# Chains between layers: one accumulator of squares, all elementwise steps on VectorE, the root read from PSUM

## The chip, the cores and the metric

The kernel runs on one core of one Trainium2 chip. The metric is the device time of one execution in microseconds, as the median of several runs.

## The reference, cut to what matters

Eight residual layers work on x of 512 tokens by 1024 features, all in float32: a pooling mixer, a conv-GeGLU feed-forward, a sliding-window attention, a second conv-GeGLU, an S5 state-space mixer, a squared-ReLU MLP, a Mamba-2 (SSD) mixer, a second MLP, and a last norm. What lies between the layers is this:

```
rms_norm(x, g)  = x * rsqrt(mean(x*x over features) + eps) * g
first four:  x = x + rms_norm(m, post_g)       # m: what the mixer or feed-forward gives
             next input = rms_norm(x, pre_g)
last four:   x = x + gate * y                  # gate, shift, scale: from a condition vector
             next input = rms_norm(x, g) * (1 + scale) + shift
```

## The kernel before, in words

x lies feature-major: eight tiles x0 to x7 of 128 features by 512 tokens. Every product is a float32 product taken as three matmuls of parts (`mm3`, lines 219 to 221): high part of the weight with high part of the activation (L219), high with low (L220), low with high (L221). A stage that makes an activation must therefore give two tiles, `hi` (ScalarE) and `lo` (the rest, VectorE). Weights are loaded in chunks and parted in the same way (L204 on ScalarE, L205 on VectorE).

`seam(before, after)` joins two layers in halves of 256 tokens: the last products of the old layer on half 0 (`tail(0)`), the chain of half 0, `tail(1)`, the chain of half 1, and then the first products of the new layer on each half (`head(0)`, `head(1)`). The chains carry a high priority. A planner that simulates the engines makes the order of each engine's queue from the program, the priorities and the waits; engines then run their queues in order.

A chain has these pieces. `Norm.add` squares a tile on ScalarE (L292 the first, L295 the others) and adds it to an accumulator; there are two accumulators, one added to by VectorE and one by GpSimd (L296), and `engs(k)` gives even tiles to VectorE and odd ones to GpSimd. `Norm.rs` sums over partitions with matmuls against ones, both accumulators into one PSUM bank (L306), takes the square root (L309) and the reciprocal (L310), puts it on diagonals (L313), spreads it over all partitions by matmuls into the other half of the bank (L319), and copies it to SBUF (L321, ScalarE). The bank comes from the pool `psn`, which has one.

`post_add` (the first four layers' ends) multiplies each tile by root and gain, `u` (L450 on VectorE; for tiles 2 and 5 a scaling on ScalarE, L442, and a product on GpSimd, L449), adds it to x (L453, alternately on VectorE and GpSimd), and, where the next norm is a `PreScale`, makes the next layer's parts of the new x without waiting for its root: `hi` (L427) and `lo` (L428). The root of `PreScale` is applied later to what the products give. `PreNorm` (before S5, both MLPs and SSD) needs the root first: x times root (L397, alternately VectorE and GpSimd), scale and shift (L400, VectorE), `hi` (L401), `lo` (L402). `staged` takes the eight tiles through these stages, each stage some tiles behind the first: 0, 2, 3, 4 in `post_add` and 0, 1, 1, 3 in `PreNorm`; it also fixes their order on each engine.

During the first seam and the first feed-forward (from about 36 to 460 us) the tables of S5 are made as background work, mostly on GpSimd, with some steps on VectorE, ScalarE and TensorE.

Of the kernel before, what the change touches and what calls it, by code (L numbers as in the profile page):

```python
# [16 lines left out]
ALU = mybir.AluOpType  # L17
# [46 lines left out]
def net_kernel(ctx: ExitStack, tc: tile.TileContext, I: dict, out: bass.AP, parts=ALL):  # L64
# [33 lines left out]
    # ---- constants  # L98
# [62 lines left out]
    # ---- x, feature-major  # L161
# [48 lines left out]
    def chunks(W, k0, nk, c0, ncol=256, kmax=4, gain=None, **kw):  # L210
        """(hi, lo, first k, k tiles) for the rows of k tiles k0.. and columns c0.. of W."""
# [19 lines left out]
    def project(W, k0, nk, c0, tiles, xh, xl, evac, **kw):  # L231
        """Output tiles (an even run of them) over all tokens; evac(n, psum, span)."""
# [8 lines left out]
    class Held:  # L241
        """Output tiles taken over one half of the tokens, then over the other; their weights stay for both.
        runs: (W, k0, nk, c0, apart, kwargs) of one or two tiles each, which share a bank; the weights of the last
        `apart` k tiles lie among the activations."""
# [20 lines left out]
        def run(self, hf, xh, xl, evac):  # L265
            """evac(run, tile of the run, psum, span)"""
# [10 lines left out]
    # ---- root mean square over features (partitions and tiles)  # L277
    class Norm:
        def __init__(self):
            self.acc = {}  # L280
            self.seen = set()

        def add(self, tile_, span, eng):
            a, b = span
            if eng not in self.acc:
                self.acc[eng] = tt("acc")
            dst = self.acc[eng][:, a:b]
            if (eng, a) not in self.seen:
                self.seen.add((eng, a))
                if span == FULL:  # L290
                    self.seen.add((eng, HALVES[1][0]))
# [6 lines left out]
        def rs(self, span, eps, out=None):  # L298
# [3 lines left out]
            accs = list(self.acc.values())  # L302
# [11 lines left out]
            if nb == 2:  # L314
                p2 = ps[:, 256:]
            else:
                p2 = psn.tile([P, 512], F32, tag="n", name=nm("pn"))
            for j in range(nb):
                T.matmul(p2[:, j * P:(j + 1) * P], ones, dg[:, j * P:(j + 1) * P], start=True, stop=True)  # L319
            out = tt("rs") if out is None else out  # L320
            A.activation(out[:, a:b], p2[:, :b - a], AF.Copy)  # L321
# [8 lines left out]
    class Line:  # L330
        """Keeps the instructions given to it in their order on their engine."""
# [1706 lines left out]
```

## Time and profile before

| What | Value |
|---|---|
| median of 3 runs | 2565.32 us (2560.61 to 2565.53) |
| span of the profiled execution, first to last instruction | 2564.4 us |
| the profiled execution's own time | the runs lie 3.8 us below to 1.1 us above its span; no time of its own is listed beside the span |
[...]
| busy share PE, DVE, ACT, POOL | 92%, 66%, 45%, 29% |

PE is TensorE, DVE is VectorE, ACT is ScalarE, POOL is GpSimd. A busy share is an average over stages with different limits; the seams are short, and what happens in them is read from the waits and the timeline there.

### The profile page before, as it was taken

Reading aid. Unit: us, or ns where it says so; the run is one execution under the profiler, and the core shown is the slowest. Engines: PE = TensorE matmul, PEld = TensorE weight load, DVE = VectorE, ACT = ScalarE, POOL = GpSimd, SP = SyncE. Lnnn points to the kernel's source line nnn. Section 1 sums busy time; section 2 is a strip of 40 time slices with the busy share of each in tenths; the row PEclk is TensorE's granted clock in tenths of the full one; section 3 lists DMA queues with packets and bytes.
Section 4 is the critical chain, followed back from the end, with each engine's and each line's share of the span. In section 5 each row is a group of like instructions: output and inputs, shape, how many; then the busy total and the mean of one; then the engine's idle time right before and its main releaser. Section 6 shows DMA issues by size and latency. Waiting matters only on the chain.

```text
span 2564.4 us, 34249 instructions
## 1 busy us (share of the span) xinstructions
PE 2368.0 (92%) x12485; PEld 1989.4 (78%) x12485; DVE 1687.6 (66%) x2739; ACT 1148.0 (45%) x2054; POOL 736.4 (29%) x1111
## 2 busy tenths in 40 slices
PE   6888996998988999996989899999999999999998
PEld 6756674887677888776878787789887888888888
DVE  6874574667857868687653667665778788633333
ACT  6533342447666544343543433334556454423332
POOL 3989988031212000004120201112043332301110
PEclk8988997999999999998989999999999999999999
DMA  4234333222155555652852255553233332233322
GB/s 121 69 98 114 118 121 101 90 80 66 33 155 158 172 181 164 197 164 76 280 180 91 82 171 185 184 172 95 88 113 106 105 98 95 84 98 99 99 86 71
DMA packets 296761, 311.34 MB, mean 121 GB/s; under 512 B 53569, under 2 KB 251025, under 8 KB 295569
## 3 DMA queue, kind: packets, MB, share of 16 engines
q1 hardware_dynamic: 267729, 274.03, 35.2%
q10 hardware_dynamic: 23680, 17.31, 2.2%
q0 software_dynamic: 5184, 17.83, 2.1%
q8 instruction: 98, 1.61, 0.3%
q14 instruction: 70, 0.57, 0.1%
HBM read 284.92 MB, written 24.18 MB: 121 GB/s over the span
## 4 chain that ended last, share of the span: by engine, by line
PE 63%; DVE 12%; POOL 9%; DMA 6%; issue 5%; ACT 4%; SPq 0%; DVEq 0%; ACTq 0%; POOLq 0%
PE mm L220 18%; PE mm L219 18%; PE mm L221 18%; DVE wl L205 3%; DMA as<-in_ada_w 3%; POOL s5buf L659 1%; ACT wh L204 1%; PE pb L1710 1%; DVE u L400 1%; PE mm L1640 1%; PE mm L1641 1%; PE mm L1642 1%; DVE lo L328 1%; PE pn L306 1%; DVE u L450 1%
## 5 line engine op out<-in xcount | busy, mean ns | idle before, releaser
L220 PE MATMUL mm<-h,wh 128*128 128x512 f32 (+1 forms) x1792 | 669.4, 374 | 26.5 <-DVE h L428 13.2
L219 PE MATMUL mm<-h,wh 128*128 128x512 f32 (+1 forms) x1792 | 665.9, 374 | 27.2 <-ACT h L401 11.4
L221 PE MATMUL mm<-h,wl 128*128 128x512 f32 (+1 forms) x1792 | 666.3, 372 | 1.9 <-DVE wl L205 1.9
L205 DVE TENSOR_TENSOR wl<-ws,wh 128x1024 fp32r<-128x1024 f32 (+1 forms) x367 | 499.5, 1365 | 252.2 <-ACT wh L204 239.4
L204 ACT ACTIVATE wh<-ws 128x1024 fp32r<-128x1024 f32 (+1 forms) x367 | 387.2, 1059 | 531.0 <-PE mm L220 435.8
L220 PEld LDWEIGHTS mm<-h,wh 128*128 128x128 f32 x1792 | 348.1, 194 | 86.4 <-DVE h L428 16.9
L219 PEld LDWEIGHTS mm<-h,wh 128*128 128x128 f32 x1792 | 348.1, 195 | 84.1 <-ACT h L401 12.6
L219 PE MATMUL mm<-hi,wh 128*128 128x512 f32 (+1 forms) x1056 | 372.7, 357 | 27.4 <-ACT hi L326 22.3
L221 PEld LDWEIGHTS mm<-h,wl 128*128 128x128 f32 x1792 | 348.7, 195 | 56.8 <-DVE wl L205 2.3
L220 PE MATMUL mm<-lo,wh 128*128 128x512 f32 (+1 forms) x1056 | 373.4, 355 | 11.8 <-DVE lo L328 11.8
L221 PE MATMUL mm<-hi,wl 128*128 128x512 f32 (+1 forms) x1056 | 373.1, 355 | 0.0
L219 PEld LDWEIGHTS mm<-hi,wh 128*128 128x128 f32 x1056 | 201.1, 191 | 55.9 <-ACT hi L326 23.9
L1264 POOL TENSOR_TENSOR r<-r 128x512 f32<-128x512 f32 x64 | 88.0, 1379 | 517.3 <-ACT r L1260 384.2
L220 PEld LDWEIGHTS mm<-lo,wh 128*128 128x128 f32 x1056 | 202.1, 191 | 40.1 <-DVE lo L328 14.2
L221 PEld LDWEIGHTS mm<-hi,wl 128*128 128x128 f32 x1056 | 202.3, 192 | 26.5
L504 DVE SCALAR_TENSOR_TENSOR aa<-as,cond,aa 128x512 f32<-128x512 f32 x168 | 130.1, 774 | 112.8 <-DMA as<-in_ada_w 111.5
L296 POOL TENSOR_TENSOR acc<-acc,sq 128x256 f32<-128x256 f32 (+1 forms) x64 | 62.1, 972 | 389.6 <-ACT sq L295 377.7
L328 DVE TENSOR_TENSOR lo<-r,hi 128x512 fp32r<-128x512 f32 x64 | 48.1, 756 | 76.4 <-ACT hi L326 76.2
L1285 DVE SCALAR_TENSOR_TENSOR x<-mm,mod,x 128x512 f32<-128x512 f32 (+1 forms) x76 | 48.9, 662 | 60.3 <-PE mm L221 60.3
L512 ACT ACTIVATE ab<-aa 128x512 bf16<-128x512 f32 x72 | 45.0, 625 | 90.6 <-DVE aa L504 50.5
L1319 POOL DMA_DIRECT2D vt<-d_tab x16 | 8.8, 555 | 264.7 <-PE mm L221 260.8
L326 ACT ACTIVATE hi<-r 128x512 fp32r<-128x512 f32 x64 | 40.2, 630 | 70.4 <-POOL r L1264 70.3
(494 smaller groups left out, 4084.5 us busy)
## 6 DMA issues: line engine op xcount, KB each, us to landing
ws<-in_mlp_w SPq DMA_DIRECT2D x124, 512.0 KB, 3.9
as<-in_ada_w SPq DMA_DIRECT2D x192, 256.0 KB, 3.1
ws<-in_ffn_w_in SPq DMA_DIRECT2D x88, 512.0 KB, 4.2
ws<-in_m_w_in SPq DMA_DIRECT2D x41, 512.0 KB, 3.7
ws<-in_ffn_w_out SPq DMA_DIRECT2D x40, 512.0 KB, 4.7
ws<-in_w_o SPq DMA_DIRECT2D x16, 512.0 KB, 3.5
ct<-d_tab SPq DMA_DIRECT2D x8, 1024.0 KB, 5.9
ws<-in_s_w_glu SPq DMA_DIRECT2D x16, 512.0 KB, 5.8
```

The lines of the kernel that those rows point to most:

```text
L204: A.activation(h_, s_, AF.Copy)
L205: V.tensor_tensor(l_, s_, f(h_), ALU.subtract)
L219: T.matmul(ps, wh, xh, start=first, stop=False)
L220: T.matmul(ps, wh, xl, start=False, stop=False)
L221: return T.matmul(ps, wl, xh, start=False, stop=last).ins
L296: eng.tensor_tensor(dst, dst, sq[:, a:b], ALU.add)
L326: hi_ = A.activation(hi[:, ts], src, AF.Copy)
L328: return hi_, V.tensor_tensor(lo[:, ts], src, f(hi[:, ts]), ALU.subtract)
L504: V.scalar_tensor_tensor(acc, st, col(k), acc, ALU.mult, ALU.add)
L512: A.activation(parts[j], acc, AF.Copy)
L1264: G.tensor_tensor(r, r, r, ALU.mult)
L1285: V.scalar_tensor_tensor(xT[n][:, ts], ps, md(i, 5, n), xT[n][:, ts], ALU.mult, ALU.add)
```

## The change

Five edits act together. (1) `Norm` keeps one accumulator, added to by VectorE alone, so the sum over partitions takes half as many matmuls. (2) `rs` returns the PSUM half-bank itself; the copy to SBUF stays only for `PreScale`, which keeps its root. (3) `post_add` does all eight products and all eight additions on VectorE, and the scalings of tiles 2 and 5 on ScalarE go. (4) `PreNorm` multiplies by root and scale in one VectorE instruction; the shift becomes the bias of ScalarE's `hi` and is added again in VectorE's `lo`, so that there are three stages instead of four. (5) The lags become 0, 1, 2, 3 and 0, 1, 2. Comments and docstrings go too.

```diff
-POST_LAGS = (0, 2, 3, 4)
-PRE_LAGS = (0, 1, 1, 3)
-POOL_K = (2, 5)
+POST_LAGS = (0, 1, 2, 3)
+PRE_LAGS = (0, 1, 2)
...
-                eng.tensor_tensor(dst, dst, sq[:, a:b], ALU.add)
+                V.tensor_tensor(dst, dst, sq[:, a:b], ALU.add)
...
-                for i, acc in enumerate(accs):
-                    T.matmul(ps[:, j * P:(j + 1) * P], acc[:, a + j * P:a + (j + 1) * P], ones,
-                             start=i == 0, stop=i == len(accs) - 1)
+                T.matmul(ps[:, j * P:(j + 1) * P], self.acc[:, a + j * P:a + (j + 1) * P], ones, start=True, stop=True)
...
-            out = tt("rs") if out is None else out
-            A.activation(out[:, a:b], p2[:, :b - a], AF.Copy)
+            out = ps[:, 256:256 + (b - a)]
             return out
...
-                return engs(k).tensor_tensor(us[k], xT[k][:, ts], rs[:, ts], ALU.mult)
+                return V.scalar_tensor_tensor(us[k], xT[k][:, ts], self.gs[:, k:k + 1], rs, ALU.mult, ALU.mult)
 
             staged((norm,
-                    lambda k: V.tensor_scalar(us[k], us[k], self.gs[:, k:k + 1], md(i, m, k), ALU.mult, ALU.add),
-                    lambda k: A.activation(self.h[k][0][:, ts], us[k], AF.Copy),
-                    lambda k: V.tensor_tensor(self.h[k][1][:, ts], us[k], f(self.h[k][0][:, ts]), ALU.subtract)),
+                    lambda k: A.activation(self.h[k][0][:, ts], us[k], AF.Identity, bias=md(i, m, k)),
+                    lambda k: V.scalar_tensor_tensor(self.h[k][1][:, ts], us[k], md(i, m, k), f(self.h[k][0][:, ts]),
+                                                     ALU.add, ALU.subtract)),
                    PRE_LAGS)
...
-            self.norm.rs(span, self.eps, out=self.rs)
+            A.activation(self.rs[:, slice(*span)], self.norm.rs(span, self.eps), AF.Copy)
...
-        for k in POOL_K:
-            A.activation(ft[k][:, ts], ft[k][:, ts], AF.Copy, scale=vc(gname, g0 + k))
...
-            if k in POOL_K:
-                return G.tensor_tensor(us[k], ft[k][:, ts], rs[:, ts], ALU.mult)
-            return V.scalar_tensor_tensor(us[k], ft[k][:, ts], vc(gname, g0 + k), rs[:, ts], ALU.mult, ALU.mult)
+            return V.scalar_tensor_tensor(us[k], ft[k][:, ts], vc(gname, g0 + k), rs, ALU.mult, ALU.mult)
...
-        staged((norm, lambda k: engs(k).tensor_tensor(xT[k][:, ts], xT[k][:, ts], us[k], ALU.add)) + parts,
+        staged((norm, lambda k: V.tensor_tensor(xT[k][:, ts], xT[k][:, ts], us[k], ALU.add)) + parts,
```

## Rows read from the trace of the kernel before

**Rows 1.** The page: the span, and the chain that ended last by engine.
```profile
span 2564.4 us, 34249 instructions
...
PE 63%; DVE 12%; POOL 9%; DMA 6%; issue 5%; ACT 4%; SPq 0%; DVEq 0%; ACTq 0%; POOLq 0%
```

**Rows 2.** Waits of PE, whole span: us in total, times, longest.
```profile
PE mm L220 <- DVE h L428: 13.2, 10, 2.7
PE mm L220 <- DVE h L402: 13.0, 10, 2.8
...
PE pn L306 <- DVE acc L296: 11.5, 5, 5.7
PE mm L219 <- ACT h L401: 11.4, 5, 2.7
PE mm L219 <- ACT h L427: 11.2, 4, 5.8
```

**Rows 3.** Timeline, seam of first MLP to SSD, half 1: start, us, instructions, idle before.
```profile
1795.35 1.13 PE L306 MATMUL pn<-ones,acc 128*128 128x128 f32 x8
...
1799.91 0.38 ACT L321 ACTIVATE rs<-pn 128x256 f32<-128x256 f32 x1 [3.13 <-PE pn L319]
1801.51 0.42 ACT L401 ACTIVATE h<-u 128x256 fp32r<-128x256 f32 x1 [1.22 <-DVE u L400]
...
1801.98 0.39 PE L219 MATMUL mm<-h,wh 128*128 128x256 f32 x1 [2.17 <-ACT h L401]
1804.19 0.39 PE L220 MATMUL mm<-h,wh 128*128 128x256 f32 x1 [1.82 <-DVE h L402]
```

**Rows 4.** Timeline of PE, seam of second feed-forward to S5, half 1.
```profile
1210.57 2.23 PE L306 MATMUL pn<-ones,acc 128*128 128x128 f32 x8 [5.21 <-DVE acc L296]
```

**Rows 5.** Timeline, seams into attention (half 1) and out of it.
```profile
573.20 0.38 ACT L321 ACTIVATE rs<-pn 128x256 f32<-128x256 f32 x1 [3.48 <-PE pn L319]
573.64 1.16 PE L306 MATMUL pn<-ones,acc 128*128 128x128 f32 x8 [0.53 <-ACT rs L321]
578.92 0.46 PE L220 MATMUL mm<-h,wh 128*128 128x256 f32 x1 [2.52 <-DVE h L428]
...
798.84 2.05 ACT L770 ACTIVATE th<-tz 128x1024 f32<-128x1024 f32 x1 [3.81 <-DMA d_tab<-th]
```

**Rows 6.** VectorE groups by line and shape: busy us, mean ns of one.
```profile
L400 DVE TENSOR_SCALAR u<-u,gs,mod 128x256 f32<-128x256 f32 x64 | 35.6, 564 | 0.3
L450 DVE SCALAR_TENSOR_TENSOR u<-f,vec,rs 128x256 f32<-128x256 f32 x48 | 32.6, 704 | 13.0 <-ACT rs L321 13.0
L296 DVE TENSOR_TENSOR acc<-acc,sq 128x256 f32<-128x256 f32 x62 | 31.7, 514 | 11.1 <-ACT sq L295 9.6
L402 DVE TENSOR_TENSOR h<-u,h 128x256 fp32r<-128x256 f32 x64 | 27.7, 451 | 0.0
L453 DVE TENSOR_TENSOR x<-x,u 128x256 f32<-128x256 f32 x32 | 20.6, 644 | 1.4 <-POOL u L449 1.4
L428 DVE SCALAR_TENSOR_TENSOR h<-x,vec,h 128x256 fp32r<-128x256 f32 x32 | 19.3, 620 | 0.7 <-ACT h L427 0.7
L397 DVE TENSOR_TENSOR u<-x,rs 128x256 f32<-128x256 f32 x32 | 18.6, 583 | 15.7 <-ACT rs L321 15.7
...
L886 DVE SCALAR_TENSOR_TENSOR dl<-mm,vec,dh 128x256 fp32r<-128x256 f32 x16 | 7.7, 479 | 3.2 <-ACT dh L885 2.9
```

**Rows 7.** Timeline of VectorE, pairs back to back, two instructions to a row.
```profile
1175.32 0.74 DVE L976 TENSOR_TENSOR f<-f,mm 128x256 f32<-128x256 f32 x2
...
1784.77 0.86 DVE L1285 SCALAR_TENSOR_TENSOR x<-mm,mod,x 128x256 f32<-128x256 f32 x2
```

**Rows 8.** Timeline of POOL in the first seam: a step of the tables.
```profile
73.50 0.29 POOL L619 TENSOR_TENSOR t<-s5k 128x64 f32<-128x64 f32 x1
```

**Rows 9.** Windows: DVE then POOL busy of L296, of L453; POOL of all lines.
```profile
73.50:96.00 22.50, 2.04 (x3) 2.59 (x4) 0.92 0.00 0
...
73.50:96.00 22.50, 2.55 (x4) 3.64 (x4) 0.92 0.00 0
...
100.00:420.00 320.00, 294.74 (x451) 0.90 0.37 111
```

More of the change, by code (lines that the diff above doesn't have):

```diff
@@ L279, in __init__, with add @@
         def __init__(self):
-            self.acc = {}
+            self.acc = None
             self.seen = set()
-        def add(self, tile_, span, eng):
+        def add(self, tile_, span):
             a, b = span
[L285 to L289, printed above, removed]
+            if self.acc is None:
+                self.acc = tt("acc")
+            dst = self.acc[:, a:b]
+            if a not in self.seen:
+                self.seen.add(a)
                 if span == FULL:
-                    self.seen.add((eng, HALVES[1][0]))
+                    self.seen.add(HALVES[1][0])
                 A.activation(dst, tile_[:, a:b], AF.Square)
@@ L295, in add, with rs @@
                 A.activation(sq[:, a:b], tile_[:, a:b], AF.Square)
[L296 to L298 removed]
+                V.tensor_tensor(dst, dst, sq[:, a:b], ALU.add)
+        def rs(self, span, eps):
             a, b = span
             nb = (b - a) // P
[L302 removed]
             ps = psn.tile([P, 512], F32, tag="n", name=nm("pn"))
             for j in range(nb):
[L305 to L307 removed]
+                T.matmul(ps[:, j * P:(j + 1) * P], self.acc[:, a + j * P:a + (j + 1) * P], ones, start=True, stop=True)
             sr = cst.tile([P, 4], F32, tag="nsr", bufs=2, name=nm("sr"))
@@ L313, in rs @@
                 V.tensor_scalar(dg[:, j * P:(j + 1) * P], ident, sr[:, j:j + 1], None, ALU.mult)
[L314 to L317, printed above, removed]
+            out = ps[:, 256:256 + (b - a)]
             for j in range(nb):
-                T.matmul(p2[:, j * P:(j + 1) * P], ones, dg[:, j * P:(j + 1) * P], start=True, stop=True)
-            out = tt("rs") if out is None else out
-            A.activation(out[:, a:b], p2[:, :b - a], AF.Copy)
+                T.matmul(out[:, j * P:(j + 1) * P], ones, dg[:, j * P:(j + 1) * P], start=True, stop=True)
             return out
@@ L447, in norm @@
             us[k] = tt("u")[:, ts]
-            if k in POOL_K:
-                return G.tensor_tensor(us[k], ft[k][:, ts], rs[:, ts], ALU.mult)
-            return V.scalar_tensor_tensor(us[k], ft[k][:, ts], vc(gname, g0 + k), rs[:, ts], ALU.mult, ALU.mult)
+            return V.scalar_tensor_tensor(us[k], ft[k][:, ts], vc(gname, g0 + k), rs, ALU.mult, ALU.mult)
         parts = pre.parts(span) if pre is not None else ()
-        staged((norm, lambda k: engs(k).tensor_tensor(xT[k][:, ts], xT[k][:, ts], us[k], ALU.add)) + parts,
+        staged((norm, lambda k: V.tensor_tensor(xT[k][:, ts], xT[k][:, ts], us[k], ALU.add)) + parts,
                POST_LAGS[:2 + len(parts)])
         for k in range(KD):
-            nxt.add(xT[k], span, engs(k))
+            nxt.add(xT[k], span)
     def reduce_angle(a, k):
@@ L912, in tail_ @@
                     A.activation(ft[n + q][:, a:b], o, AF.Copy, scale=vc("pool_scale", n + q))
-                    sq.add(ft[n + q], (a, b), engs(q))
+                    sq.add(ft[n + q], (a, b))
             if hf == 0:
@@ L977, in down @@
                 if last:
-                    S_["sq"].add(ft[n], span, engs(n))
+                    S_["sq"].add(ft[n], span)
         def body_():
@@ L1142, in o_proj @@
                     A.activation(ft[n + q][:, slice(*HALVES[th])], o, AF.Copy)
-                    S_["sq"].add(ft[n + q], HALVES[th], engs(q))
+                    S_["sq"].add(ft[n + q], HALVES[th])
         def head(hf, pre):
@@ L1286, in down @@
             if nxt is not None:
-                nxt.add(xT[n], span, engs(n))
+                nxt.add(xT[n], span)
             bg[0](1)
@@ L1426, in glu @@
             if S_["nxt"] is not None:
-                S_["nxt"].add(xT[n], span, engs(n))
+                S_["nxt"].add(xT[n], span)
         def body_():
@@ L1666, in o_evac @@
             if S_["nxt"] is not None:
-                S_["nxt"].add(xT[n], span, engs(n))
+                S_["nxt"].add(xT[n], span)
         def bcast(a, o, d=64):
@@ L1893, in chain @@
             for k in range(KD):
-                nxt.add(xT[k], span, engs(k))
+                nxt.add(xT[k], span)
     work = Background()
```

2 lines of the change are left out of this document (removed).

## Prediction

> **What bounds the kernel now.** I read first the page's chain of waits: TensorE carries 63% of it and stands at 92% busy, VectorE 12% and POOL 9% [rows 1]. So over most of the span only matmul work counts, and nothing of that changes. The change can be worth no more than the places where TensorE stands still for a chain between layers. The second view, the waits of TensorE alone, gives their size: 13.2 us for `lo` and 11.2 for `hi` of the parts made behind `post_add`, 13.0 for `lo` and 11.4 for `hi` of `PreNorm`, 11.5 for the accumulator of squares, together 60.3 us in 34 waits [rows 2]. That is the most that shorter chains can remove directly, 2.4% of the span.
>
> The third view is the timeline of one seam, half 1 of MLP to SSD [rows 3]. The reader is to see the order: sum matmuls, then the root's copy to SBUF at 1799.91, the first `hi` at 1801.51, TensorE's first product at 1801.98, and its second, which needs the first `lo`, only at 1804.19. TensorE is idle 2.17 + 1.82 us of these 4.3. So what ends last is the first `lo`, and that is VectorE's: before it stand products, scalings and waits for GpSimd's share. The fourth view, the groups by line, shows what the two engines do to each other: VectorE's plain additions and products have means of 514 to 704 ns in the lines that run beside GpSimd, while the same shapes back to back, with GpSimd idle, take 0.37 us (two in 0.74) and, with a scalar pointer, 0.43 us (two in 0.86) [rows 6, 7].
>
> **The change part by part.** The base is the profiled execution, 2564.4 us; the median of the runs lies 0.9 us above, which I add at the end.
>
> *PreNorm.* Removed are the copy of the root (0.38 us), the separate scaling, and GpSimd's products. In the new order VectorE does product 0, 1, 2 and then `lo` 0: with 0.43 us for each product and 0.48 for the last, 1.8 us, and 0.1 for the hand-over, 1.9 us from the point at which the copy now starts [rows 6, 7]. ScalarE's `hi` 0 takes 0.42 us now [rows 3]; even if its new bias makes it half as long again, it ends 0.43 + 0.1 + 0.63 = 1.2 us on, before the turn of `lo` 0 at 1.3. Against 4.3 us now the gain is 2.4 us a half. Five halves wait like this, as the count of the `hi` row says, and a sixth (SSD to second MLP) for `lo` alone [rows 2]: 6 x 2.4 = 14.4 us. What comes after the first `lo` stays as it was: a tile now costs VectorE 2 x 0.43 = 0.86 us, before half a product and two others at 0.37, 0.93. The lower bound is that the later tiles set the end, at 8 x 0.07 = 0.6 us plus the 0.4 of the copy, 1.0 a half, 6 us; the upper is all of both `PreNorm` rows, 24.4.
>
> The product now reads the root from PSUM, and no row shows that product. The nearest is L886, the same instruction with an operand in PSUM, at 479 ns [rows 6], and L1285's pair in rows 7, also from PSUM; I take them, and so charge nothing more. [...]
>
> *post_add.* With lags 0, 1, 2, 3 VectorE does four products (1.72 us), three additions (1.11) and `lo` 0 (0.48): 3.3 us from the root. Into attention it is 5.7 now, from 573.20 to 578.92 [rows 5], so 2.4 us for this half. Out of attention the longest wait for `hi`, 5.8 us [rows 2], is not GpSimd's: ScalarE's queue stands behind a copy of the S5 tables that waits 3.81 us for a DMA [rows 5]. Nothing of the change touches that, so between 0 and 2.4 I take 1.2. The first half into attention I put at nothing, since `head` work covers most of it. Sum 3.6; bounds 0 and 24.4, the rows' whole.
>
> *Second feed-forward to S5* has `post_add` and `PreNorm` one behind the other, so the whole first chain is bare. TensorE waits 5.21 us for the accumulator and then takes 2.23 us for eight sum matmuls, four of which go [rows 4]: 1.1, and 0.4 for the copy, 1.5 a half, 3.0 for both. VectorE's additions that were GpSimd's I put at nothing, since GpSimd's ended no earlier; the bound is all 11.5 us of rows 2.
>
> *Sums of squares elsewhere.* Eight sum matmuls take 1.13 us [rows 3], half of it goes: 0.5 us in the six other halves counted above, 3.0. Where TensorE would have waited anyway it is nothing: 0 to 3.
>
> *VectorE's load.* This is the cover of all that, so it has to be checked. The seven lines of rows 6 without L886 cost VectorE 186.1 us. After the change there are, by the program's loops, 128 products, 96 `lo` with a pointer among those lines, 64 additions to x and 148 to accumulators (168 squares less 20 first ones). At 0.43 and 0.37: 224 x 0.43 + 212 x 0.37 = 175 us. VectorE takes over all of GpSimd's share and yet ends no fuller, if the means of rows 6 fall to rows 7's. If they stay, 224 x 0.62 + 212 x 0.51 = 247 us, 61 more, and half of that in waits would eat the gains.
>
> *First seam.* The chain of waits runs on POOL from there to 416 us: POOL is busy 294.74 of the 320 us after 100 [rows 9], and TensorE waits for its tables in the first feed-forward. So I count nothing for this seam's own waits, but what GpSimd loses of it once the tables' steps have begun, at 73.50 [rows 8]: 2.59 us of accumulating and 3.64 of additions [rows 9], 6.2 us. Against it, VectorE's own table steps, which must come first, stand behind more chain work of high priority: I take 2 us off and keep 4.2; bounds -6 and 10. No queue of SP or POOL gets a new DMA, and no DMA moves.
>
> Sum: 14.4 + 3.6 + 3.0 + 3.0 + 4.2 = 28.2 us. 2564.4 - 28.2 = 2536.2, and with 0.9, **2537 us**.
>
> **The rivals.** *The bank is held.* The root now lies in the only bank of its pool until the eighth product has read it: eight products, some six additions and four `lo` later, 8 x 0.43 + 6 x 0.37 + 4 x 0.43 = 7.4 us, where the copy freed it after 0.4. In the three seams with `PreScale` the next root's sums stand right behind: into attention they started at 573.64, 0.53 us behind the copy, ahead of the new layer's products in TensorE's queue [rows 5]. If the planner leaves them there, TensorE waits 7.4 us where 3.3 would have done: 4 us more in three seams, 12 us, and the time is 2549. Against it: the planner sees the wait and can queue the products first.
>
> *The chains end sooner than TensorE's other waits show.* Waits shorten by more, because with GpSimd gone nothing doubles VectorE's instructions (means of 514 to 704 against 370 and 430): twice the two first terms, 18 us more, and 2519.
>
> *Slower: the tables lose their pace.* Every queue is planned anew. POOL's work from 100 to 420 us is on the chain; it idles 25 us there [rows 9]. If VectorE's and ScalarE's steps for it come later in their queues, because chain work goes ahead, its idle time grows and each microsecond is one of the kernel's. This decides above 24 us of new idle time, the sum without the first seam: about twice what it idles now. At 35 the time is 2565.3 - 24 + 35 = 2576.
>
> **How the numbers follow.** The forecast, with its own range 2526 to 2547: 0.52. The held bank (2547 to 2558): 0.18. The larger gain (2508 to 2526): 0.16. The tables' loss, slower: 0.11; the same with a loss that just cancels: 0.03. A difference under 0.2%, 5 us, is about what a measurement of this kernel can't tell from none. Of the held bank nearly all is still faster. So faster 0.84, same 0.05, slower 0.11. The range goes from 2510, where half of all 60 us is gone and the tables gain too, to 2559, which takes in the held bank and leaves out the tables' loss.
>
> **What would show it.** Right: TensorE's waits for `lo` behind `PreNorm` shrink from 13.0 to under 6, the first `lo` comes some 2 us after the spread of the root, VectorE's chain lines have means near 0.4 to 0.5 us, and the sum matmuls stand four to a root instead of eight. Wrong for the first seam: POOL's work on the tables does not end earlier. The held bank would show as a wait of the sum matmuls for the last product. The prediction is wrong as a whole if VectorE's means stay at 0.5 to 0.7 without GpSimd beside it, or if TensorE's idle time moves from the seams into the first feed-forward.

## The result, and the profile after

The changed kernel takes 2526.39 us (median of 4 runs, 2522.45 to 2528.71) against 2563.69 us of the kernel before beside it: a ratio of 0.9855, 95% interval 0.9841 to 0.9868, so 37 us or 1.45% faster. The forecast was 2537 us, in a range of 2510 to 2559.

The page of the changed kernel, its span and the chain of waits by engine. VectorE has the same share as in [rows 1]; POOL fell from 9% to 7%.

```profile
span 2525.6 us, 33954 instructions
...
PE 66%; DVE 12%; POOL 7%; DMA 6%; issue 4%; ACT 4%; SPq 0%; DVEq 0%; ACTq 0%; POOLq 0%
```

TensorE's waits over the whole span (us in total, times, longest). They answer to [rows 2]: L392 and L391 are the remainders and rounded parts of `PreNorm` (13.0 and 11.4 before), L419 and L418 those behind `post_add` (13.2 and 11.2 before), L303 the sum matmuls (11.5 before). L312 are the matmuls that spread the root; in the kernel before their row is the last one here.

```profile
PE pn L303 <- DVE acc L295: 17.8, 2, 9.4
PE pn L312 <- DVE dg L309: 12.2, 8, 4.4
...
PE mm L218 <- ACT h L418: 8.0, 4, 2.4
...
PE mm L219 <- DVE h L419: 7.5, 10, 1.4
PE mm L218 <- ACT h L391: 7.0, 6, 1.5
...
PE mm L219 <- DVE h L392: 3.1, 5, 1.2
```

```profile
PE pn L319 <- DVE dg L313: 2.5, 3, 1.0
```

The reader is to see three things. The four rows for rounded parts and remainders fell from 48.8 us to 25.6. The wait for the accumulator grew by 6.3, and that for the diagonals, which no term of the forecast has, by 9.7. Together these rows went from 62.8 us to 55.6. So most of the gain is not in the waits that these rows list, and TensorE's idle and busy time have to be looked at as a whole. The pages have them, before and then changed:

```profile
PE 2368.0 (92%) x12485; PEld 1989.4 (78%) x12485; DVE 1687.6 (66%) x2739; ACT 1148.0 (45%) x2054; POOL 736.4 (29%) x1111
```

```profile
PE 2346.8 (93%) x12397; PEld 1970.7 (78%) x12397; DVE 1686.3 (67%) x2839; ACT 1143.1 (45%) x2022; POOL 611.5 (24%) x967
```

Of the 38.8 us between the two profiled executions TensorE's idle time gives 17.6 (196.4 to 178.8) and its busy time 21.2. The busy time fell for two reasons. There are 88 sum matmuls fewer, four in each of 22 roots; at 1.13 us for eight and 0.61 for four, as the seam below has them, that is an estimate of 11 us. And the mean granted clock rose from 0.962 to 0.967: by the trace's clock records TensorE did 128 us of its work at the lower of the two levels that they hold, 0.50 of full speed and 1.00, before and 104 now, 109 in a second execution told of below. In the kernel before, 128x256 matmuls start 0.21 us apart at 0.50 (13 steps from 1436.16 to 1438.93) and 0.12 apart at 1.00 (13 from 1440.02 to 1441.58), so some 0.44 of that difference, an estimate of 8 to 11 us, is what it is worth. The clock is not that of one execution alone: the runs of the kernel before beside the later experiments have 0.959 to 0.962, the eight of the changed kernel 0.965 to 0.969. Span and mean granted clock of the two profiled executions, before and then changed:

```profile
core 0: 2564.4 us, clock 0.962
```

```profile
core 0: 2525.6 us, clock 0.967
```

The timeline of the seam from the first MLP to SSD, half 1, as in [rows 3]:

```profile
1764.60 0.61 PE L303 MATMUL pn<-ones,acc 128*128 128x128 f32 x4
...
1766.18 0.68 PE L312 MATMUL pn<-dg,ones 128*128 128x128 f32 x4 [0.96 <-DVE dg L309]
1766.90 1.26 DVE L388 SCALAR_TENSOR_TENSOR u<-x,gs,pn 128x256 f32<-128x256 f32 x3 [0.67 <-PE pn L312]
1767.41 1.30 ACT L391 ACTIVATE h<-u,mod 128x256 fp32r<-128x256 f32 x3 [1.90 <-DVE u L388]
...
1767.97 0.39 PE L218 MATMUL mm<-h,wh 128*128 128x256 f32 x1 [1.11 <-ACT h L391]
...
1768.61 0.39 PE L219 MATMUL mm<-h,wh 128*128 128x256 f32 x1 [0.25 <-DVE h L392]
```

From the point where the root is there to TensorE's second product it was 4.28 us (1799.91 to 1804.19) and is 1.71 (1766.90 to 1768.61). From the start of the sums to that product it was 8.84 and is 4.01; but in the kernel before TensorE had products of the other half to do between sums and spread, so that difference is not all idle time.

The timeline of the seam from the second feed-forward to S5, half 1, against [rows 4]: the spread of `post_add`'s root, VectorE's additions, and the sum matmuls. The wait for the accumulator is 9.40 us, where it was 5.21.

```profile
1185.53 0.60 PE L312 MATMUL pn<-dg,ones 128*128 128x128 f32 x4
...
1192.34 3.06 DVE L295 TENSOR_TENSOR acc<-acc,sq 128x256 f32<-128x256 f32 x6
...
1195.54 1.20 PE L303 MATMUL pn<-ones,acc 128*128 128x128 f32 x4 [9.40 <-DVE acc L295]
```

The spread of the same root in the kernel before:

```profile
1200.45 0.60 PE L319 MATMUL pn<-dg,ones 128*128 128x128 f32 x4
```

VectorE's groups by line (busy us, mean ns), against [rows 6]. The means of products and additions to x have fallen from 583 to 704 ns to 438 to 474.

```profile
L295 DVE TENSOR_TENSOR acc<-acc,sq 128x256 f32<-128x256 f32 (+1 forms) x148 | 63.7, 443 | 16.2 <-ACT sq L294 11.9
...
L392 DVE SCALAR_TENSOR_TENSOR h<-u,mod,h 128x256 fp32r<-128x256 f32 x64 | 29.9, 479 | 0.2 <-ACT h L391 0.2
L434 DVE SCALAR_TENSOR_TENSOR u<-f,vec,pn 128x256 f32<-128x256 f32 x64 | 29.6, 472 | 7.5 <-PE pn L312 7.5
L388 DVE SCALAR_TENSOR_TENSOR u<-x,gs,pn 128x256 f32<-128x256 f32 x64 | 29.0, 474 | 9.1 <-PE pn L312 9.1
L437 DVE TENSOR_TENSOR x<-x,u 128x256 f32<-128x256 f32 x64 | 28.0, 438 | 0.0
L419 DVE SCALAR_TENSOR_TENSOR h<-x,vec,h 128x256 fp32r<-128x256 f32 x32 | 16.4, 518 | 1.1 <-ACT h L418 1.1
```

The first seam: the step of the tables that [rows 8] has at 73.50, the VectorE step that it waits for, and a later pair of the tables.

```profile
66.21 0.21 DVE L597 TENSOR_TENSOR s5k<-s5k,t 128x64 f32<-128x64 f32 x1
66.50 0.41 POOL L603 TENSOR_TENSOR t<-s5k 128x64 f32<-128x64 f32 x1 [8.28 <-DVE s5k L597]
...
82.64 2.35 POOL L709 TENSOR_TENSOR cp<-cc,s5k 128x512 f32<-128x512 f32 x2
```

In the kernel before:

```profile
68.13 5.40 POOL L296 TENSOR_TENSOR acc<-acc,sq 128x256 f32<-128x256 f32 x4 [1.98 <-ACT sq L295]
70.37 0.21 DVE L613 TENSOR_TENSOR s5k<-s5k,t 128x64 f32<-128x64 f32 x1
...
95.80 2.18 POOL L725 TENSOR_TENSOR cp<-cc,s5k 128x512 f32<-128x512 f32 x2
```

The pair stood at 95.80 and stands at 82.64, so the tables are 13.2 us ahead: 7.0 by an earlier start, 6.2 because nothing of the chain lies between. The earlier start has two parts. VectorE's step comes 4.2 us sooner (70.37 to 66.21), and behind it GpSimd's step waited 3.1 us for the four additions of squares that stood in GpSimd's queue, where now it starts within 0.3.

**Where the time came from.** For each VectorE and ScalarE instruction that stands in both programs (the n-th of its line) I took how much earlier it starts than in the kernel before; the gain at a point is the median over those within 15 us of it, and a stretch's gain the difference of two points. The forecast's terms stand with the stretch of their halves. The fourth column is a second profiled execution of the changed kernel, the other three are runs told of below. All in us; the ends of the stretches are times in the kernel before.

| stretch | forecast | changed | again | spare additions | four stages | sums on TensorE |
|---|---|---|---|---|---|---|
| first seam and first feed-forward, to 540 | 4.2 | 13.0 | 13.2 | 3.9 | 13.0 | 19.8 |
| into attention, to 610 | 2.9 | 4.3 | 4.6 | 5.5 | 5.6 | 7.9 |
| attention, out of it, second feed-forward, to 1150 | 1.7 | -1.4 | -8.8 | -5.8 | -6.5 | 0.4 |
| into S5, to 1250 | 7.8 | 1.5 | 2.5 | 1.5 | -0.5 | 12.6 |
| S5, to 1395 | 0 | 4.0 | 6.3 | 6.0 | 4.9 | 1.6 |
| S5 to first MLP, to 1500 | 5.8 | 8.2 | 8.0 | 8.3 | 3.2 | 6.1 |
| first MLP, to 1740 | 0 | 1.9 | 0.3 | -0.5 | -2.0 | -0.4 |
| first MLP to SSD, to 1850 | 2.9 | 5.0 | 5.7 | 4.9 | 4.6 | 5.2 |
| SSD, to 2150 | 0 | -0.9 | -5.1 | -1.3 | 0.9 | -3.0 |
| SSD to second MLP, to 2320 | 2.9 | 3.3 | 3.3 | 3.2 | -1.4 | 0.9 |

The seams agree between the two executions of one program within 1 us. The stretches that the change does not touch differ by up to 7.4 us, so a seam's row can be read to about a microsecond, and the others say little.

TensorE's idle time in a stretch is steadier; in the four seams below the two executions differ by 0.2 us at most. It is the length less TensorE's busy time, in us, the ends of a stretch moved by each run's gain at that point, and stands here for the four seams with `PreNorm`, in the kernel before, the changed kernel, and the runs told of below. In the three seams behind S5 it fell by 9.0 us, of the 16.5 that the table above gives them; the rest is busy time.

| run | into S5 | S5 to first MLP | first MLP to SSD | SSD to second MLP |
|---|---|---|---|---|
| before | 20.8 | 8.6 | 5.3 | 4.6 |
| changed | 21.9 | 3.9 | 2.5 | 3.1 |
| again | 21.9 | 3.9 | 2.3 | 3.1 |
| GpSimd's share back | 15.9 | 3.9 | 1.9 | 3.2 |
| root copied | 23.4 | 4.4 | 3.0 | 4.7 |
| four stages | 23.7 | 6.5 | 3.2 | 5.4 |
| old lags | 22.3 | 4.7 | 2.7 | 4.0 |
| two accumulators | 18.7 | 4.2 | 2.3 | 3.1 |
| root whole | 23.6 | 6.2 | 3.5 | 4.2 |
| sums on TensorE | 9.4 | 6.1 | 3.7 | 4.7 |
| root by place | 9.4 | 3.9 | 2.4 | 3.1 |

### The profile page after: what moved, and what is told of

Read it like the earlier page. It is cut to its first block, busy times and chain, and to the rows that moved or that the text cites. A ratio compares the mean times of both kernels' runs of the same rounds, so it can differ in the third digit from the quotient of the medians.

```text
span 2525.6 us, 33954 instructions
## 1 busy us (share of the span) xinstructions
PE 2346.8 (93%) x12397; PEld 1970.7 (78%) x12397; DVE 1686.3 (67%) x2839; ACT 1143.1 (45%) x2022; POOL 611.5 (24%) x967
## 4 chain that ended last, share of the span: by engine, by line
PE 66%; DVE 12%; POOL 7%; DMA 6%; issue 4%; ACT 4%; SPq 0%; DVEq 0%; ACTq 0%; POOLq 0%
PE mm L219 20%; PE mm L218 19%; PE mm L220 19%; DVE wl L204 3%; DMA as<-in_ada_w 2%; ACT wh L203 1%; PE mm L1624 1%; PE mm L1625 1%; DMA d_tab<-s5buf 1%; PE mm L1626 1%; POOL s5buf L642 1%; POOL s5buf L644 1%; PE pb L1694 1%; DVE aa L488 1%; POOL s5buf L643 1%
## 5 line engine op out<-in xcount | busy, mean ns | idle before, releaser
L219 PE MATMUL mm<-h,wh 128*128 128x512 f32 (+1 forms) x1792 | 665.3, 372 | 11.1 <-DVE h L419 7.5
L204 DVE TENSOR_TENSOR wl<-ws,wh 128x1024 fp32r<-128x1024 f32 (+1 forms) x367 | 479.5, 1309 | 254.0 <-ACT wh L203 239.0
L488 DVE SCALAR_TENSOR_TENSOR aa<-as,cond,aa 128x512 f32<-128x512 f32 x168 | 131.5, 783 | 109.0 <-DMA as<-in_ada_w 107.7
L295 DVE TENSOR_TENSOR acc<-acc,sq 128x256 f32<-128x256 f32 (+1 forms) x148 | 63.7, 443 | 16.2 <-ACT sq L294 11.9
```

The source lines that it names most:

```text
L204: V.tensor_tensor(l_, s_, f(h_), ALU.subtract)
L219: T.matmul(ps, wh, xl, start=False, stop=False)
L295: V.tensor_tensor(dst, dst, sq[:, a:b], ALU.add)
L488: V.scalar_tensor_tensor(acc, st, col(k), acc, ALU.mult, ALU.add)
```

## The experiments

Ratios are to the kernel before, beside which each ran.

**The changed kernel again.** No edit.

> The changed kernel once more, word for word, as a second execution under the profile and a base on the same chip for the others: 2526 us within 4. Where a stage that no edit touches (the feed-forwards' bodies, S5's body, attention) differs between the two profiles by 2 us, such a difference elsewhere says nothing about an edit. If instead the stages agree within 1 us, differences of 2 us and more between kernels come from the new order of the queues.

Measured: 2533.18 us against 2568.13, ratio 0.9868 (0.9852 to 0.9884). The time is 7 us above the first, outside the 4 expected; the kernel before is 4.4 us slower beside it too, and the ratios agree. The two profiles agree within 0.3 us until 540 us and end 8.8 us apart (the bottom of the table's columns adds to 38.9 and 30.0), so the first reading holds: differences of a few us inside the bodies say nothing. Where the second execution loses most, from 610 to 1150 us of the kernel before, TensorE is idle 3.5 us longer and busy 4.1 us longer, and the granted clock of the stretch is 0.97 where the first has 0.98. Part of the idle time goes with longer waits for weights: between 880 and 1010 us VectorE waits 24.4 us for them (L488) where the first has 21.8.

For the other runs I take 0.9862, between the two ratios of the changed kernel, as the base; 0.0010 is 2.6 us, and a run's interval is some 0.0016 to either side.

**GpSimd's share back, everywhere.** `eng` is `engs` of the tile, and each engine has an accumulator of its own.

```diff
-                V.tensor_tensor(dst, dst, sq[:, a:b], ALU.add)
+                eng.tensor_tensor(dst, dst, sq[:, a:b], ALU.add)
...
+    def engs(k, first=False):
+        return G if k % 2 and (True if first else True) else V
...
-    staged((norm, lambda k: V.tensor_tensor(xT[k][:, ts], xT[k][:, ts], us[k], ALU.add)) + parts,
+    staged((norm, lambda k: engs(k, first).tensor_tensor(xT[k][:, ts], xT[k][:, ts], us[k], ALU.add)) + parts,
```

> The changed kernel with GpSimd's odd share back in every seam: additions to x and additions of squares of odd tiles, with a second accumulator and eight sum matmuls a root instead of four. PreNorm's stages, the products of post_add and the root in PSUM stay as changed. Theory (the share that left GpSimd is worth something only ahead of the tables and in the sum matmuls; the seams gain by their shorter chains on VectorE): the first seam gives back about 12 us, the sums 3 us, and the second feed-forward to S5 gains up to 7 us, since its two accumulators run side by side (TensorE's wait for the accumulator falls from 9.4 us to about 5): 2526 + 15 - 7 = 2534 us. Rival (the two engines slow each other, and that was the larger part of the gain in all seams): the lines of VectorE go back to means of 500 to 700 ns and all but the folded stages is lost, 2526 + 25 = 2551 us or more.

Measured: 2541.47 us, ratio 0.9897 (0.9884 to 0.9910), some 9 us slower than the changed kernel, between the theory's loss of 8 and the rival's of 25. The profile has both signs: the first feed-forward ends 9.8 us later than in the changed kernel (gain there 3.2 us), and into S5 it gains 5.1 us instead of 1.5, with the shorter wait that was expected. The rival's sign shows too, in part: of VectorE's groups the additions of squares go to a mean of 549 ns (514 before, 443 changed) and the remainders behind `post_add` to 730 (620 and 518), but the products, which read PSUM, stay at 472 and 474. TensorE's row for the accumulator, whole span:

```profile
PE pn L306 <- DVE acc L296: 11.5, 2, 6.4
```

**The same share back in the first seam alone.** The edit is shown against the run before it.

```diff
-        return G if k % 2 and (True if first else True) else V
+        return G if k % 2 and (True if first else False) else V
```

> The changed kernel with GpSimd's odd share (additions to x and of squares, second accumulator) back in the first seam alone, between the pooling layer and the first feed-forward. Theory (GpSimd's queue: this share stood among the tables' steps, and the tables set the end until they are done): the tables' first steps start late again and all of it is lost later, some 12 of the 38.8 us: 2538 us, with the loss complete by 222 us of the span. Rival (the prediction's own term, 4.2 us): 2530 us. Rival (the first seam gained by the shorter chain on VectorE, not by GpSimd's queue): no change, 2526 us.

Measured: 2530.50 us, ratio 0.9859 (0.9847 to 0.9872): no loss in the time. In the profile the loss is there by 540 us, 3.3 us gained instead of 13.0; it then gains 6.1 into attention and 3.3 from there to 840, where the changed kernel has 4.3 and -2.1. So the stage reading was right, and the expected loss of 12 us in the time did not come.

**Spare additions on GpSimd in the first seam.** VectorE's chain stays as changed; GpSimd adds in place, on squares and products that are already used.

```diff
                 V.tensor_tensor(dst, dst, sq[:, a:b], ALU.add)
+                if extra:
+                    spare(sq[:, a:b])
...
+    def spare(src):
+        G.tensor_tensor(src, src, src, ALU.add)
...
+            if first and k % 2:
+                spare(us[k])
```

> The changed kernel with extra additions on GpSimd in the first seam, as many and as large as its share there before (additions of odd squares and to odd tiles of x), whose results nobody reads; VectorE's chain is as changed. Theory (GpSimd's queue: these instructions stand ahead of and among the tables' steps): by the end of the first feed-forward (540 us) 7 to 10 us of the gain there of 12.5 us are lost, as in the run with GpSimd's share back in the first seam. Rival (that run lost by the longer chain through two engines): by 540 us at most 2 us are lost, and the time is 2526 us.

Measured: 2540.39 us, ratio 0.9898 (0.9881 to 0.9915), 9 us slower. By 540 us 3.9 us are gained instead of 13.0. VectorE waits for none of their results, so the rival falls: the loss needs no longer chain through two engines. POOL's timeline, the same two steps as above:

```profile
69.78 0.41 POOL L615 TENSOR_TENSOR t<-s5k 128x64 f32<-128x64 f32 x1 [0.56 <-DVE s5k L609]
...
96.56 4.15 POOL L721 TENSOR_TENSOR cp<-cc,s5k 128x512 f32<-128x512 f32 x2
```

The pair is back at 96.56, near where the kernel before has it. Of the 13.9 us, 10.6 lie between the two steps, in GpSimd's queue, which is more than the 6.2 that the kernel before had there; 3.3 are a later start. That start is VectorE's: the step that this one waits for also comes 3.3 us later than in the changed kernel (69.48 against 66.21). Why this run keeps the loss to the end and the one before it does not is open.

**The root copied.**

```diff
-            out = ps[:, 256:256 + (b - a)]
+            p2 = ps[:, 256:256 + (b - a)]
...
+            out = tt("rs")[:, a:b] if out is None else out
+            A.activation(out, p2, AF.Copy)
             return out
```

> The changed kernel with the root copied to SBUF by ScalarE again, ahead of the products of PreNorm and post_add. Theory (the copy stood bare on the chain): 0.4 us for each of 8 halves of PreNorm and some 4 of post_add, 2526 + 3 to 5 = 2530 us. Rival (the root's bank, held until the eighth product, costs as much in sums that wait for it as the copy): 2526 us, and TensorE's waits for the spread of the next root get shorter. Second rival (a product that reads PSUM takes longer): means of the product lines fall below those of the changed kernel and the time is 2524 us.

Measured: 2536.42 us, ratio 0.9882 (0.9868 to 0.9897), about 5 us slower by the ratio, as the theory had it, though its interval overlaps that of the changed kernel's second measurement. TensorE's idle time bears it out: 4.1 us more in the four seams with `PreNorm`. The second rival falls by VectorE's groups: the two products, now from SBUF, have the means of the changed kernel, 484 and 478 ns against 472 and 474.

```profile
L436 DVE SCALAR_TENSOR_TENSOR u<-f,vec,rs 128x256 f32<-128x256 f32 x64 | 30.4, 484 | 8.6 <-ACT rs L314 8.6
L390 DVE SCALAR_TENSOR_TENSOR u<-x,gs,rs 128x256 f32<-128x256 f32 x64 | 29.3, 478 | 11.8 <-ACT rs L314 11.8
```

**Four stages again.**

```diff
-    V.scalar_tensor_tensor(us[k], xT[k][:, ts], self.gs[:, k:k + 1], rs, ALU.mult, ALU.mult)
+    V.tensor_tensor(us[k], xT[k][:, ts], rs, ALU.mult)
...
+    lambda k: V.tensor_scalar(us[k], us[k], self.gs[:, k:k + 1], md(i, m, k), ALU.mult, ALU.add),
-    lambda k: A.activation(self.h[k][0][:, ts], us[k], AF.Identity, bias=md(i, m, k)),
+    lambda k: A.activation(self.h[k][0][:, ts], us[k], AF.Copy),
...
-               PRE_LAGS)
+               (0, 1, 1, 3))
```

> The changed kernel with PreNorm's four stages and their lags 0, 1, 1, 3 as before (product with the root, scale and shift, rounded part, remainder), but all of VectorE's on VectorE. Theory (the fold is what brought the first remainder forward): eight instructions of 0.4 us stand ahead of and with the first remainder instead of four, 1.7 us more for each of 6 to 8 halves and TensorE waits for the remainder again as in the kernel before: 2526 + 10 to 14 = 2538 us. Rival (the move away from GpSimd did it, the fold little): 2528 us.

Measured: 2547.14 us, ratio 0.9922 (0.9908 to 0.9936), 15 us slower: the largest of the single steps. In the table 2 to 3 us are lost into S5, 5 from S5 to the first MLP, 4.7 from SSD to the second MLP. TensorE's idle time in the four seams with `PreNorm` is 7.4 us longer. The clock has a share in the rest: in the last of these seams 0.98 is granted, where the changed kernel has 1.00. TensorE's waits, whole span, `PreNorm` only (7.0 and 3.1 in the changed kernel):

```profile
PE mm L218 <- ACT h L392: 10.0, 6, 1.9
PE mm L219 <- DVE h L393: 8.0, 9, 1.8
```

**The old lags.**

```diff
-POST_LAGS = (0, 1, 2, 3)
-PRE_LAGS = (0, 1, 2)
+POST_LAGS = (0, 2, 3, 4)
+PRE_LAGS = (0, 1, 3)
```

> The changed kernel with every later stage one tile further behind: lags 0, 2, 3, 4 in post_add and 0, 1, 3 in PreNorm, so that another product stands ahead of the first remainder. Theory (the order of the queue sets the first remainder): 0.4 us more in each of 8 halves of PreNorm and some 4 of post_add, 5 us, 2531 us, with TensorE's waits for remainders up by as much. Rival (VectorE's rate over all eight tiles sets the end, not the first remainder): 2526 us.

Measured: 2541.44 us, ratio 0.9887 (0.9870 to 0.9904), 6.5 us slower, near the theory's 5, with an interval that overlaps the changed kernel's second one. TensorE's idle time in the four seams with `PreNorm` grows by 2.3 us only. `PreNorm`'s wait for remainders rises from 3.1 to 5.8 us; the rows behind `post_add` show no such rise, so the whole of it is not accounted for.

The four single steps that were undone cost 9, 5, 15 and 6.5 us, together 36 us, about what the changed kernel gains. That they add up so well is in part luck. Each figure has an interval of some 4 us to either side; the four stages and the old lags both set the remainder back by the same lag; GpSimd's share brings the second accumulator and its sum matmuls with it; and GpSimd's products, in `PreNorm` and for tiles 2 and 5, were not undone at all.

**Two accumulators, both VectorE's, into S5.** `two` is set there alone.

```diff
+            w = k % 2 if self.two else 0
-            dst = self.acc[:, a:b]
+            dst = self.acc[w][:, a:b]
```

> The changed kernel with two accumulators between the second feed-forward and S5, both VectorE's, odd and even tiles apart, and eight sum matmuls a root there. Theory (additions into one accumulator take longer because each waits for the one before it: six in 3.0 us, 0.51 us each, against 0.37 us for two that are independent): six take 2.2 us and TensorE's wait for the accumulator falls from 17.8 to about 16 us; the sums give most of it back, 2526 us within the noise. Rival (the additions take that long because of the squares that they read, or of other work): the spacing stays at 0.5 us and the wait at 17.8.

Measured: 2536.81 us, ratio 0.9871 (0.9855 to 0.9888), no change, as expected. The mechanism shows in VectorE's timeline of half 0, and in TensorE's wait:

```profile
1161.92 0.76 DVE L296 TENSOR_TENSOR acc<-acc,sq 128x256 f32<-128x256 f32 x2
1165.71 1.43 DVE L296 TENSOR_TENSOR acc<-acc,sq 128x256 f32<-128x256 f32 x4
```

```profile
PE pn L306 <- DVE acc L296: 14.6, 2, 7.8
```

Four additions into two accumulators take 1.43 us, 0.36 each; six into one took 3.06, 0.51 each. The wait falls by 3.2 us, and eight sum matmuls (2.05 us instead of 1.20) give part of it back. The time between the spread of `post_add`'s root and the sums, half 1, is 8.37 us (1187.11 to 1195.48), where the changed kernel has 10.01.

**The root made whole.** A version that goes further, since the waits for the accumulator and the diagonals were now the longest of the chains.

```diff
-            for j in range(nb):
-                T.matmul(ps[:, j * P:(j + 1) * P], self.acc[:, a + j * P:a + (j + 1) * P], ones, start=True, stop=True)
...
+            T.matmul(ps[:, :b - a], ones, self.acc[:, a:b], start=True, stop=True)
+            out = tt("rs")[:, a:b] if out is None else out
+            A.activation(out, ps[:, :b - a], AF.Sqrt, bias=eps, scale=1.0 / D)
+            V.reciprocal(out, out)
```

> The changed kernel with the root made on all partitions at once: one sum matmul with the ones as the weight gives every token's sum on all 128 partitions, ScalarE takes the square root of 128 x 256 from PSUM into SBUF and VectorE its reciprocal there; the two scaled diagonals and the matmuls that spread them go, and the products read SBUF. Theory (after the change, what ends last in the seams is the root's own chain: TensorE waits 12.2 us for diagonals and the path from the sums to the spread is some 2.2 us): about 1 us off in each of 10 to 12 halves, 2526 - 10 = 2516 us, and no waits for diagonals. Rival (a reciprocal over 256 columns costs VectorE as much as the steps it replaces): 2526 us. Second rival (it costs 2 us and more): 2535 us.

Measured: 2521.86 us against 2533.18 of the changed kernel on the same chip; ratio 0.9825 (0.9809 to 0.9840). The 11 us are the theory's, but not in the places it named. The seams of `PreNorm` alone get worse: 6.4, 4.5 and 1.3 us gained over the kernel before, where the changed kernel has 8.2, 5.0 and 3.3; TensorE is idle 4.4 us longer in them. The gain lies ahead of them, 17.8 us by 540 and 7.6 into attention; what of it is the earlier free bank and what the new order of the queues was not tried.

**The sums on TensorE, into S5.**

```diff
+            if self.bank is not None:
+                sq = tt("sq")
+                A.activation(sq[:, a:b], tile_[:, a:b], AF.Square)
+                T.matmul(self.bank[:, :b - a], ones, sq[:, a:b], start=k == 0, stop=k == KD - 1)
+                return
```

> As the run with the whole root, and between the second feed-forward and S5 the squares of the new x are summed by TensorE, eight matmuls into one bank, in place of VectorE's chain of additions into one accumulator. Theory (the single accumulator is what kept this seam from gaining: its additions follow each other at 0.5 us and TensorE waited 17.8 us for it, 11.1 before): the wait falls under 10 us, this seam gains 4 to 7 us over the run with the whole root, 2510 us. Rival (the products and the additions to x end last there, the accumulator only follows them): under 2 us, 2515 us.

Measured: 2514.35 us, ratio 0.9792 (0.9777 to 0.9807), 7.5 us better than the run with the whole root. Into S5 it gains 12.6 us, where that run gains 3.7. TensorE's waits in that seam (1115 to 1200 us), and VectorE's group of the reciprocals:

```profile
PE mm L218 <- ACT h L390: 6.8, 2, 3.4
PE pn L287 <- ACT sq L286: 2.3, 2, 1.4
```

```profile
L311 DVE RECIPROCAL rs<-rs 128x256 f32<-128x256 f32 x16 | 28.0, 1751 | 36.5 <-ACT rs L310 36.5
```

The rival falls: the wait of 17.8 us for the accumulator has become one of 2.3 for squares. Not all of the gain is that wait, though: TensorE, with the sums to do, is idle 9.4 us in this seam instead of 23.6, and the granted clock of the stretch is 0.96, where the run with the whole root has 0.86. What each of the two is worth was not separated. The 1751 ns of the reciprocal is what stands bare in the other seams.

**The root by place.** `PreNorm`'s three seams without `post_add` go back to diagonals.

```diff
-            rs = self.norm.rs(span, self.eps)
+            rs = self.norm.rs(span, self.eps, whole=self.norm.bank is not None)
```

> The run with the sums on TensorE, but PreNorm's root in the three seams without post_add (S5 to the first MLP, MLP to SSD, SSD to the second MLP) made by diagonals again, as in the changed kernel; elsewhere the root is made whole. Theory (the 1.75 us that the reciprocal over 128 x 256 takes stands bare in those three seams, where the path by two diagonals is shorter): those seams go back from 6.1, 2.9 and 1.2 us gained over the kernel before to the changed kernel's 8.1, 5 and 3.2: 6 us, 2514 - 6 = 2508 us. Rival (the diagonals' two small steps and their hand-overs cost as much as the reciprocal): 2514 us.

Measured: 2513.59 us, ratio 0.9782 (0.9767 to 0.9797). The three seams gain 7.5, 5.0 and 3.2 us instead of 6.1, 5.2 and 0.9, which is 3.5 us and not 6, and the time does not tell this run from the one before. TensorE's idle time falls by 5.1 us there, as the theory has it, and is that of the changed kernel again. It is the fastest measured: 2.2% under the kernel before and, by the ratios 0.9862 and 0.9782, 0.8% under the changed kernel.

## Why the prediction was right in sum, and where its terms were wrong

The forecast sum was 28.2 us and the gain 36 to 37, inside the range. That it came so near is in part luck: the first seam gave 9 us too much, the seam into S5 6 us too little, and an estimated 8 to 11 us go with the clock, for which the forecast has no term. Term by term:

*PreNorm, right in mechanism, with the sums too small and the clock left out.* Forecast: 1.9 us from the root to the first remainder's product; measured 1.71, a gain of 2.57 us against 2.4. The run that undoes the fold alone costs 15 us, most of it in these seams. In the three seams of `PreNorm` alone TensorE's idle time fell by 9.0 us, where four halves of 2.4, 9.6, were forecast. It is not 2.4 in each: in half 1 of MLP to SSD the idle time behind the sums fell from 3.99 us to some 2.5, as TensorE now waits 0.96 for the diagonals, where products of the other half had covered that path. But the three seams gained 16.5 us, where 11.6 were forecast with the sums. What is left is busy time. The sum matmuls were counted in eight halves at 0.5 to 1.1 us; they went in all 22, and count wherever TensorE is the bound, an estimate of 11 us in all against the 5.2 of the sum. The rest goes with the clock: in the three seams 0.95, 0.98 and 0.99 of full speed were granted before (1395 to 1500, 1740 to 1850 and 2150 to 2320 us), and 0.98, 0.98 and 1.00 are in the same stretches of the changed kernel.

The half from 1425 us of the kernel before, in the seam from S5 to the first MLP, shows it. Behind two waits of 1.82 and 1.72 us it went on in part at the lower of the clock's two levels, 0.50 from 1436 to 1439 us and 0.89 in the mean of 15 us; the same half of the changed kernel waits 1.11 us ahead of its products and the granted clock stays at 1.00. The windows (PE, PEld, DVE, ACT, POOL busy, clock, DMA), before and then changed:

```profile
1425.00:1440.00 15.00, 11.45 (x79) 10.84 (x79) 9.07 (x23) 4.85 (x14) 3.29 (x4) 0.89 0.00 1
```

```profile
1403.00:1418.00 15.00, 13.75 (x110) 13.30 (x110) 9.39 (x21) 8.41 (x17) 1.38 (x1) 1.00 0.05 8
```

The same is seen inside S5, where nothing of the change lies and 4.0 us were gained. The stretch, before and then changed:

```profile
1250.00:1395.00 145.00, 132.56 (x769) 117.53 (x768) 75.32 (x90) 62.41 (x84) 23.39 (x35) 0.94 0.59 186
```

```profile
1232.60:1373.60 141.00, 128.76 (x766) 113.98 (x765) 78.06 (x93) 62.16 (x84) 20.32 (x33) 0.96 0.60 192
```

TensorE is idle 12.4 and 12.2 us; the 4 us are busy time, at a clock of 0.94 and 0.96. The second execution has 0.98 there and gains 6.3; the run with the root by place has 0.94 and gains nothing. So the gain inside S5 goes with the clock. Why the clock stood higher there is open.

*The first seam: 4.2 us forecast, 13 found, beyond the upper bound of 10.* The failed step is "what GpSimd loses of it once the tables' steps have begun, at 73.50". It counted the 6.2 us of chain work behind that point, which the trace confirms to the tenth, and nothing ahead of it; but the start itself went from 73.50 to 66.50. Of these 7.0 us, 2.8 are GpSimd's additions of squares that stood ahead of the step, and 4.2 are VectorE's own table step, for which the forecast had taken 2 us off: it came earlier, not later. The spare additions show that work in GpSimd's queue takes the gain back, without a longer chain. How much of the 9 us reaches the end is less sure, since one of the two runs that take it back lost it and the other did not.

*Into S5: 7.8 us forecast, 1.5 and 2.5 found.* The failed step is "VectorE's additions that were GpSimd's I put at nothing, since GpSimd's ended no earlier". Two engines had summed side by side; now VectorE does all seven after its products, and each waits for the last, six of them 0.51 us apart. TensorE's wait went from 11.5 us, nearly all of it in this seam, to 17.8: 6.3 more, by which the term falls short. The chain itself did not get longer in half 1: from the spread of `post_add`'s root to the sums it took 10.12 us (1200.45 to 1210.57) and takes 10.01 (1185.53 to 1195.54). What the copy and the shorter instructions gave back, the additions took; and the wait grew because 4.3 us of TensorE's work that had stood behind the spread now stand ahead of it. In half 0 the same stretch grew from 14.96 us (1166.20 to 1181.16) to 17.35 (1149.73 to 1167.08). Three runs show from three sides that the accumulator is what is waited for: GpSimd's half back, 11.5; two accumulators, 14.6; sums on TensorE, 2.3. What the new order of TensorE's queue alone costs was not tried.

*post_add: right in sign.* Into attention 2.9 us with the sums, found 4.3 and 4.6. Out of attention nothing can be read, since that stretch differs more between two executions of one program than the term's 1.7 us.

*VectorE's load: wrong, without effect.* The lines of the chain cost 186.1 us before and 196.6 now (63.7, 29.9, 29.6, 29.0, 28.0 and 16.4), not 175. The means fell, to 438 to 518 ns, but not to the 370 and 430 of back-to-back pairs. Half of a pair's time is not the mean of one instruction: a single addition shows 0.41 us, and a second begins 0.33 after it. Nor was GpSimd idle beside the first pair of [rows 7]: its addition ran from 1175.47 to 1176.20, and VectorE's pair reads one of its operands from PSUM.

*The rivals.* The held bank did not come: no row has sum matmuls waiting for a product, and with the bank freed early by the copy the kernel is slower. The tables did not lose pace, they gained. The larger gain, by faster VectorE instructions, is half true: the means did fall, and the time, 2526, lies at the edge between that case and the forecast's own range. On reading the root from PSUM, the row of L886 with its 479 ns was right, and there was nothing more to charge: the products take 472 and 474 ns from PSUM, 484 and 478 from SBUF.

Open: why the clock stood higher inside S5, the order of TensorE's queue into S5, and the end of the run with GpSimd's share in the first seam alone.

## What to carry to other kernels

Price a change at the bound engine by its idle time and its busy time apart: here 21.2 of the 38.8 us gained were busy time, matmuls that went and a clock that was granted more, and the list of waits shows neither. When work leaves an engine that later feeds the bound, count the time by which that engine's next chain can start, not only what lies inside it. When two engines' sums become one, the additions turn from two short chains into one serial one, and where that chain stands bare it can take back all that fewer instructions give, as into S5, where TensorE's wait for it went from 11.1 to 17.8 us. A seam is shortened by everything between its first sum and the first product, so measure it from end to end before and after, not by the wait that shows last.

## What was not expected of the hardware

In the kernel before, two of VectorE's chain lines took 1.7 and 1.8 times as long in the mean with GpSimd at work beside them as alone; the products that read the root from PSUM, in a run with GpSimd's share back, did not. By the single instructions of the kernel before, 25 of VectorE's 32 additions to x (L453) ran while a GpSimd instruction ran and took 708 ns in the mean, the other 7 took 411; of the 48 products of root and gain (L450), with the root in SBUF, 31 beside GpSimd took 831 ns and 17 alone 473. The same product with the root in PSUM, in the run with GpSimd's share back everywhere (L442), takes 472 ns in 30 cases beside GpSimd and in 34 alone.

Additions into one accumulator follow each other at 0.51 us (six in 3.06), independent ones of the same shape at 0.36 (four in 1.43), while a single one shows 0.41 to 0.42: in these rows an addition begins before the one ahead of it has ended only where it does not need that one's result.

VectorE's reciprocal took longer the wider it was: in the changed kernel a mean of 161 ns for 128x2 (L306), 545 for 128x64 (L590) and 946 for 128x128 (L1536), and 1751 for 128x256 with the sums on TensorE. From the start of the square root to the first product it is 2.30 us that way (1175.63 to 1177.93, into S5 with the sums on TensorE) and 1.65 by diagonals and a spread (1765.25 to 1766.90, the changed kernel).

Two executions of one program, equal to 0.3 us over the first 540 us, ended 8.8 us apart. Some of it goes with the granted clock: from 610 to 1150 us of the kernel before it was 0.98 in the one and 0.97 in the other, and TensorE was busy 4.1 us longer.
